# Feed-forward gate and up as seven block products, down in three passes, on a two-block network (one Trainium2 core)

## Chip, core and metric

The kernel runs on one core of a Trainium2 chip. The metric is the device time of one execution in microseconds (us). An execution's engines are TensorE (PE), VectorE (DVE), ScalarE (ACT), GpSimd (POOL) and SyncE (SP, which here issues DMAs).

## What is computed

The input is 1024 tokens of 1024 floats (fp32), and there are two blocks. The first has a mixer (a convolution branch and a recurrent branch, merged and multiplied by w_o) and a gated feed-forward part; the second has two further mixers and 32 experts. The part that the change touches, from the reference (D_FF is 2816):

```python
x = x + merged @ w_o[l]
h = rmsnorm(x, ln2_g[l])
x = x + (jax.nn.silu(h @ w_ffn_gate[l]) * (h @ w_ffn_up[l])) @ w_ffn_down[l]
return rmsnorm(x, final_g)
```

## The kernel before

**Numbers.** Each fp32 operand of a matrix product is held as a high and a low part of 12 bits (`split`: the high part is an ACT copy, L56, the low part a DVE subtraction, L57), and a product is three fp32r matmuls (`mm3`, L87 to L89: high x high, high x low, low x high). A weight tile of 1 MB is loaded by SP into one of two `raw` buffers, and its split units come from a pool of five.

**Stages.** `stage1` is the first mixer, in two halves of 512 tokens (`hf`); its last product, w_o, adds the residual and stores the sum x2 to DRAM (`x2d`). `prep` then norms token tiles of 128 (`norm`, L124 to L126, with `rstd`, whose power runs on POOL, L117) and transposes them (`to_T`, L135 on PE, L138 on ACT, L139 on DVE) to operands of 512 tokens, `xT` and `x2T`. `stage2` is the feed-forward part, `stage4` the mixers of the second block, `stage5` the experts.

**Feed-forward.** 2816 columns are 22 tiles of 128. `gates()` and `ups()` take two of them at a time: per column tile and token half one `col` of 8 k-tiles x 3 matmuls of 128x512, that is 96 per pair of tiles. The gate's tanh (L446, ACT), its product (L447, DVE) and the product with up (L462, DVE) give the hidden tile, which is split at once (L463 ACT, L464 DVE) and stays in SBUF. `down()` multiplies each pair of hidden tiles with two rows of w_ffn_down, for all eight token tiles and both halves of the columns, and L482 (DVE) adds each result to the residual `xh` in SBUF: 160 additions. The last two pairs go by halves of the tokens, with the final norm (`finish`, L489 and L491) and the next stage's transposes between them. The order of the work on each engine is set by the scheduler of the framework from the order in which the program is written.

```python
            sg = gates()
            for t in range(0, NFF - 4, 2):
                hid = ups(sg)
                sg = gates()
                down(hid, down_units(t), range(8))
```

Of the kernel before, what the change touches and what calls it, by code (L numbers as in the profile page):

```python
# [31 lines left out]
class Net:  # L32
# [39 lines left out]

    def n_units(self, w, r0, nk, c0):
        """Row tiles of w, 512 columns from c0, two row tiles a unit."""
# [9 lines left out]
    def mm3(self, out, w, x, first, last):  # L84
        """out += w^T x, both as (high, low) pairs; w is the one held in the array."""
# [5 lines left out]
    def col(self, ps, unit, xT, n0=0, n=HT):  # L91
        """ps [128 columns, n tokens] = unit^T xT"""
# [7 lines left out]
    def pair(self, slot, name):  # L100
        """A (high, low) pair [128, 8, 512] in one of the two large slots."""
# [8 lines left out]
    def rstd(self, pool, ssq, n, scale=1.0):  # L110
        """(scale * ssq / n + eps) ^ -0.5 for [128, m]"""
# [8 lines left out]
    def norm(self, pool, x, gB, out):  # L120
        """out = rmsnorm(x) * g for a natural tile [128, 1024]"""
# [7 lines left out]
    def to_T(self, psp, xn, dst, t0, nk=KD, k0=0, tag="tp"):  # L129
        """dst (high, low) [:, k, t0:t0+128] = xn[:, k*128:(k+1)*128]^T"""  # L130
# [10 lines left out]
    def rows_T(self, psp, wk, tmp, specs, name, tag="tp"):  # L141
        """Vectors of DRAM, as rows of 128, turned to columns: {name: [128, n] AP}."""
# [17 lines left out]
    def stage1(self):  # L160
        tc, nc, a = self.tc, self.nc, self.a
        self.x2d = self.dram.tile([S, D], F32, name="x2d")
        with ExitStack() as ctx:
# [3 lines left out]
            pst = ctx.enter_context(self.pool(name="s1pt", bufs=2, space=PSUM))  # L167

            def t(name):
                return wk.tile([P, HT], F32, tag="t", name=name, bufs=11)  # L170
# [49 lines left out]
            # softplus(-lambda)  # L220
# [6 lines left out]
            # block-diagonal maps of the heads 2c, 2c + 1 for c of a pair  # L227
# [11 lines left out]

            for hf in range(2):  # L240
                T0 = hf * HT

                # short convolution branch
                ya = self.pair(1 - hf, "ya")
                for c in range(0, 8, 2):
                    cs = []
                    for j, u in enumerate(self.t_units(w_in, [D + c * P, D + c * P + P])):
# [17 lines left out]
                    for j, u in enumerate(self.t_units(w_in, [c * P, c * P + P])):  # L265
# [3 lines left out]
                        self.put(ya, c + j, cs[j])  # L269

                if hf == 0:
                    self.route_const()
                pa = mid.tile([P, 8, HT], F32, tag="pa", name="pa")
# [12 lines left out]
                # recurrent branch  # L286
                yb = self.pair(1 - hf, "yb")
                for c in range(0, 8, 2):
# [25 lines left out]
                    def gates():  # L314
                        for j in range(2):
# [7 lines left out]
                            # x = -log a = 4 sp (1 + tr);  1 - a = (1 + e^-x) tanh(x / 2)  # L323
# [7 lines left out]
                        # sqrt(1 - a^2) = (1 + a) sqrt(tanh(x / 2))  # L331
# [23 lines left out]
                thb = mid.tile([P, 8, HT], F32, tag="thb", name="thb")  # L355
# [12 lines left out]
                # the next transposed input is made while the last product runs  # L368
                xT = self.pair(1 - hf, "xT")
                if hf == 0:  # L370
                    prep(lambda tt: load(a["x"][0, HT + tt * P:HT + (tt + 1) * P, :], nc.gpsimd), a["ln1_g"][0], xT)
                else:
                    prep(lambda tt: load(self.x2d[tt * P:(tt + 1) * P, :], nc.gpsimd), a["ln2_g"][0], xT)
                    x2n = mid.tile([P, 4, D], F32, tag="pa", name="x2n")
                for ch in range(2):
# [6 lines left out]
                    for tt in range(4):  # L382
                        r0 = T0 + tt * P
                        cs = slice(ch * 512, (ch + 1) * 512)
                        xr = x2n[:, tt, cs] if hf else t("xr")
# [3 lines left out]
            self.x2T = [xT, self.pair(1, "x2T")]  # L389
            prep(lambda tt: x2n[:, tt], a["ln2_g"][0], self.x2T[1])  # L390

    def put(self, dst, k, src):
        """dst (high, low) [:, k] = src"""
# [4 lines left out]
    def softplus(self, tmp, out, x, sgn, bias=0.0):  # L398
        """out = log(1 + exp(y)), y = sgn * x + bias; tmp() gives a tile like out."""
# [5 lines left out]
        # log1p(e) = 2 atanh(z), z = e / (2 + e) <= 1/3  # L405
# [11 lines left out]
    def stage2(self):  # L417
        tc, nc, a = self.tc, self.nc, self.a
        with ExitStack() as ctx:
            hp = ctx.enter_context(self.pool(name="s2hid", bufs=4))  # L420
            wk = ctx.enter_context(self.pool(name="s2wk", bufs=2))
            psp = ctx.enter_context(self.pool(name="s2ps", bufs=6, space=PSUM))
            pst = ctx.enter_context(self.pool(name="s2pt", bufs=2, space=PSUM))
            self.resc = ExitStack()
            self.res = self.resc.enter_context(self.pool(name="res", bufs=1, side="right"))
            res1 = ctx.enter_context(self.pool(name="res1", bufs=1, side="right"))
            self.x1h = self.res.tile([P, 4, D], F32, tag="xh", name="xh0")
            xh1 = res1.tile([P, 4, D], F32, name="xh1")
            xres = [self.x1h[:, t] for t in range(4)] + [xh1[:, t] for t in range(4)]
            self.x1d = self.dram.tile([HT, D], F32, name="x1d")  # L430
            xT = self.x2T
            for t in range(8):
                nc.gpsimd.dma_start(xres[t], self.x2d[t * P:(t + 1) * P, :])
            wd = a["w_ffn_down"][0]
            gg = self.t_units(a["w_ffn_gate"][0], [t * P for t in range(NFF)])
            gu = self.t_units(a["w_ffn_up"][0], [t * P for t in range(NFF)])

            def gates():
                sg = []
                for _ in range(2):  # L440
                    u = next(gg)
                    for hf in range(2):
                        ps = psp.tile([P, HT], F32, tag="acc", name="acc")
                        self.col(ps, u, xT[hf])
                        th = wk.tile([P, HT], F32, tag="th", name="th", bufs=4)
                        nc.scalar.activation(th, ps, AF.Tanh, scale=0.5)  # L446
                        nc.vector.scalar_tensor_tensor(th, th, 1.0, ps, op0=ALU.add, op1=ALU.mult)  # L447
                        sg.append(th)
                return sg

            def ups(sg):
                hid = []
                for j in range(2):
                    u = next(gu)
                    ht = hp.tile([P, 2, S], F32R, tag="hid", name="hid")
                    hid.append(ht)
                    for hf in range(2):
                        s = slice(hf * HT, (hf + 1) * HT)
                        ps = psp.tile([P, HT], F32, tag="acc", name="acc")
                        self.col(ps, u, xT[hf])  # L460
                        th = sg[2 * j + hf]
                        nc.vector.tensor_tensor(th, th, ps, ALU.mult)  # L462
                        nc.scalar.activation(ht[:, 0, s], th, AF.Copy)  # L463
                        nc.vector.tensor_tensor(ht[:, 1, s], th, ht[:, 0, s].bitcast(F32), ALU.subtract)  # L464
                return hid

            def down_units(t):
# [1077 lines left out]
```

## Time and profile before

| what | value |
|---|---|
| time, median of 3 runs | 3396.74 us (3393.51 to 3402.04) |
| span of the profiled execution | 3397.5 us |
| PE busy | 3230.0 us, 95% |
| DVE, ACT, POOL busy | 2072.2, 1419.9, 609.1 us |
| PE's granted clock, most slices | 1.0 |

The profiled execution is 0.8 us longer than the median of the runs; the page gives no time for it but its span. The stages follow one another; the feed-forward block fills about 950 to 1667 us. A busy share is a mean over all stages, so for each claim the rows of its own stretch are read.

### The profile page before, as it was taken

To read this page: it belongs to the slowest core of one execution; us is meant where nothing else is said; L and a number is where in the kernel's file an instruction comes from. 1 tells how busy PE (TensorE), PEld (TensorE's weight loads), DVE (VectorE), ACT (ScalarE), POOL (GpSimd) and SP (SyncE) were. 2 spreads that over 40 slices of the span, in tenths; PEclk is the share of its full clock that TensorE was granted. 3 is DMA by queue.
4 is the path that set the end of the run, shared out by engine and by line. 5 is a ranking of instruction groups with operands and counts; after the bars stand their busy time and mean duration, and the time that the engine had idled before them with its cause. 6 is when DMAs were issued, how large, how long until landed. Compare 5 with 4: busy or idle time off the path is not lost. (4 is left out here: it accounts for less than half of the span.)

```text
span 3397.5 us, 39631 instructions
## 1 busy us (share of the span) xinstructions
PE 3230.0 (95%) x15457; PEld 2661.3 (78%) x15457; DVE 2072.2 (61%) x2869; ACT 1419.9 (42%) x1954; POOL 609.1 (18%) x649
## 2 busy tenths in 40 slices
PE   8999999999999999999999999899999899999993
PEld 6887888877778888888777888777888778878772
DVE  5437544365544334333787665877656678888886
ACT  3227432255321111111343333443443378878873
POOL 0002210011210000000232111132112143334433
PEclk9999999999999999999999999999999899999996
DMA  4332433323431111111323323243332699969993
GB/s 154 99 100 85 145 118 99 99 85 117 136 118 50 50 50 38 62 50 35 105 88 106 103 91 92 73 145 109 103 109 93 230 322 384 381 256 389 368 349 155
DMA packets 313080, 487.81 MB, mean 144 GB/s; under 512 B 28400, under 2 KB 190460, under 8 KB 311868
## 3 DMA queue, kind: packets, MB, share of 16 engines
q1 hardware_dynamic: 291532, 427.02, 36.5%
q0 software_dynamic: 19488, 51.44, 4.2%
q10 hardware_dynamic: 1872, 6.82, 0.5%
q8 instruction: 122, 2.00, 0.2%
q14 instruction: 66, 0.54, 0.0%
HBM read 465.65 MB, written 36.34 MB: 148 GB/s over the span
## 5 line engine op out<-in xcount | busy, mean ns | idle before, releaser
L57 DVE TENSOR_TENSOR unit<-raw,unit 128x1024 fp32r<-128x1024 f32 x682 | 887.0, 1321 | 434.1 <-ACT unit L56 427.1
L56 ACT ACTIVATE unit<-raw 128x1024 fp32r<-128x1024 f32 x746 | 775.8, 1057 | 770.7 <-PE acc L89 689.5
L87 PE MATMUL acc<-xT,unit 128*128 128x512 f32 x1712 | 679.3, 397 | 0.1
L88 PE MATMUL acc<-xT,unit 128*128 128x512 f32 x1712 | 672.2, 393 | 0.0
L89 PE MATMUL acc<-xT,unit 128*128 128x512 f32 x1712 | 670.3, 392 | 0.0
L87 PEld LDWEIGHTS acc<-xT,unit 128*128 128x128 f32 x1712 | 323.7, 189 | 68.7 <-issue 1.2
L88 PEld LDWEIGHTS acc<-xT,unit 128*128 128x128 f32 x1712 | 323.4, 189 | 68.4 <-issue 3.6
L89 PEld LDWEIGHTS acc<-xT,unit 128*128 128x128 f32 x1712 | 323.2, 189 | 68.2 <-issue 1.0
L88 PE MATMUL gu<-unit,xT 128*128 128x512 f32 x512 | 207.3, 405 | 16.7 <-POOL unit L57 9.5
L87 PE MATMUL gu<-unit,xT 128*128 128x512 f32 x512 | 207.2, 405 | 1.1 <-ACT xT L138 0.8
L89 PE MATMUL gu<-unit,xT 128*128 128x512 f32 x512 | 204.5, 400 | 0.0
L88 PE MATMUL acc<-unit,xT 128*128 128x256 f32 (+1 forms) x640 | 196.4, 307 | 2.0 <-DVE unit L57 2.0
L87 PE MATMUL acc<-unit,xT 128*128 128x256 f32 (+1 forms) x640 | 193.9, 308 | 3.1 <-ACT xb L709 3.0
L89 PE MATMUL acc<-unit,xT 128*128 128x256 f32 (+1 forms) x640 | 195.4, 306 | 0.0
L57 POOL TENSOR_TENSOR unit<-raw,unit 128x1024 fp32r<-128x1024 f32 x64 | 157.7, 2464 | 156.8 <-issue 89.9
L482 DVE SCALAR_TENSOR_TENSOR xh<-acc,xh 128x512 f32<-128x512 f32 x160 | 110.4, 690 | 85.1 <-PE acc L89 84.5
L87 PE MATMUL acc<-unit,hid 128*128 128x512 f32 x352 | 137.3, 390 | 0.0
L89 PE MATMUL acc<-unit,hid 128*128 128x512 f32 x352 | 137.2, 390 | 0.0
L87 PE MATMUL acc<-x2T,unit 128*128 128x512 f32 x352 | 137.1, 389 | 0.1
L88 PE MATMUL acc<-unit,hid 128*128 128x512 f32 x352 | 137.1, 389 | 0.0
L88 PE MATMUL acc<-x2T,unit 128*128 128x512 f32 x352 | 136.9, 389 | 0.0
L89 PE MATMUL acc<-x2T,unit 128*128 128x512 f32 x352 | 136.9, 389 | 0.0
(425 smaller groups left out, 5641.0 us busy)
## 6 DMA issues: line engine op xcount, KB each, us to landing
raw<-in_w_in_dram SPq DMA_DIRECT2D x104, 1024.0 KB
raw<-in_exp_w_gate_dram SPq DMA_DIRECT2D x64, 1024.0 KB
raw<-in_exp_w_up_dram SPq DMA_DIRECT2D x64, 1024.0 KB
raw<-in_exp_w_down_dram SPq DMA_DIRECT2D x64, 1024.0 KB
raw<-in_w_ffn_gate_dram SPq DMA_DIRECT2D x11, 1024.0 KB
raw<-in_w_ffn_up_dram SPq DMA_DIRECT2D x11, 1024.0 KB
raw<-in_w_ffn_down_dram SPq DMA_DIRECT2D x11, 1024.0 KB
raw<-in_w_out_dram SPq DMA_DIRECT2D x9, 1024.0 KB
```

What stands on the lines that cost most here:

```text
L56: nc.scalar.activation(h, src, AF.Copy)
L57: (low or nc.vector).tensor_tensor(l, src, h.bitcast(F32), ALU.subtract)
L87: mm(out, w[0], x[0], start=first, stop=False)
L88: mm(out, w[0], x[1], start=False, stop=False)
L89: mm(out, w[1], x[0], start=False, stop=last)
L482: nc.vector.scalar_tensor_tensor(xs, ps, 0.5, xs, op0=ALU.mult, op1=ALU.add)
```

## The change

**Gate and up by block products.** The product of a pair of column tiles with all tokens is cut 2x2x2 (two halves of k, two column tiles, two token halves) and made from seven products of half the k each, instead of eight: sums of weight blocks (`b_blocks`, L459 to L471, five additions of 128x512 on POOL per pair) are multiplied with sums of token blocks, and the results are put together by DVE additions on 128x512 (`vadd`, L644). The seven are called m1 to m7; they take 7 x 4 x 3 = 84 matmuls. Some accumulate into a bank that another has filled (L642). The order of the steady loop: m1 and m6 of a pair, m4 of the pair before it (into the bank of its m7), m2, m3 of the pair before, m5, m7, with the splits of the next pair's weights between. `use` makes tanh and products (L659, L660, L663); the hidden tiles are stored to DRAM (`hidD`, by the ACT queue, 44 DMAs of 256 KB).

**Early tokens.** The first 512 tokens are normed, transposed and summed during the second half of stage 1 (`early`), and their six blocks are kept in DRAM (`eD`, 24 stores of 256 KB) and read back in stage 2 (six loads of 1 MB).

**w_o of the later tokens** moves to stage 2: eight PSUM banks for four token tiles x two column halves; k-tiles 0 to 3 for all of them first, then 4 to 7 tile by tile (`last`), each tile followed by its norm (`norm_a` to `norm_c`) and its transposes and sums (`turn`, L606 to L627; the low parts of the sums on POOL, L618).

**Down** comes after all of gate and up, in three passes over token tiles 0 to 2, 3 to 5 and 6 to 7: each accumulates all 22 k-tiles in PSUM, reads the hidden tiles and all of w_ffn_down again, and adds the residual once (L867, 16 additions). `finish` of a pass is followed by the transposes for stage 4 in the next.

```diff
-            def gates():
-                        self.col(ps, u, xT[hf])
-            def down(hid, us, tts):
-                        nc.vector.scalar_tensor_tensor(xs, ps, 0.5, xs, op0=ALU.mult, op1=ALU.add)
...
+        def sums(names):
+            t, T, V = t2()
+            if names == ("T2", "T1"):
+                g(V, B12, B11, ALU.subtract)
+                g(T, B22, V, ALU.subtract)
+            elif names == ("T3", "T4"):
+                g(T, B22, B12, ALU.subtract)
+                g(V, B21, T, ALU.subtract)
+                g(V, V, B11, ALU.subtract)
...
+                def m1(m):
+                    m.A = acc()
+                    prod(m.A, m.b["B11"], x["A11"], True)
+                    m.s1 = st("s1")
+                    nc.scalar.activation(m.s1, m.A, AF.Copy)
+                def m2(m):
+                    prod(m.A, m.b["B21"], x["A12"], False)
+                    m.use(0, m.A)
+                def m4(m):
...
+                        prod(m.B, m.b["T4"], x["A22"], False)
+                        vadd(m.s1, m.s1, m.B)
+                        m.use(2, m.s1)
+                def m5(m):
+                    m.C = acc()
+                    prod(m.C, m.b["T1"], x["S1"], True)
+                def m6(m):
+                    m.B = acc()
+                    prod(m.B, m.b["T2"], x["S2"], True)
+                    m.u2 = st("u2")
+                    vadd(m.u2, m.s1, m.B)
+                def m7(m):
+                    prod(m.B, m.b["T3"], x["S3"], False)
+                    m.u3 = st("u3")
+                    vadd(m.u3, m.s1, m.B)
...
+                    vadd(m.u3, m.u3, m.C)
+                    m.use(3, m.u3)
+                def m3(m):
+                    prod(m.C, m.b["B22"], x["S4"], False)
+                    vadd(m.u2, m.u2, m.C)
+                    m.use(1, m.u2)
...
+            last(2, 0)
+            t = turn(0)
+            for _ in t:
+                pass
+            last(2, 1)
+            rs[2] = norm_a(2)
+            last(3, 0)
+            t = turn(1)
+            next(t)
+            norm_b(2)
+            next(t)
+            norm_c(2, rs[2])
+            last(3, 1)
...
+            for n in range(3, NFF + 1):
+                q = Mat(n, ths) if n < NFF else None
+                m.m1()
+                m.m6()
+                if p:
+                    p.m4()
+                m.split()
+                m.m2()
+                if p:
+                    p.m3()
+                if q:
+                    q.split(2)
+                m.m5()
+                if q:
+                    q.split()
+                m.m7()
+                p, m = m, q
+            p.m4()
+            p.m3()
...
+            for tts in ((0, 1, 2), (3, 4, 5), (6, 7)):
+                n = len(tts)
+                accs = [[acc() for _ in range(2)] for _ in tts]
+                for f in range(0, NFF, 2):
+                    hr = hp.tile([P, 2, n * P], F32, tag="hr", name="hr", bufs=2)
+                    nc.sync.dma_start(hr, self.hidD[f * P:(f + 2) * P, t0:t0 + n * P].rearrange("(k p) t -> p k t", p=P))
+                    raw = self.raw_p.tile([P, 2, D], F32, tag="raw", name="raw")
+                    nc.sync.dma_start(raw, wd[f * P:(f + 2) * P, :].rearrange("(k p) c -> p k c", p=P))
```

**The order on the engines.** DVE before, in the feed-forward loop, from one pair's down splits over the products of up to the gates of the next:

```order
L57 TENSOR_TENSOR unit_6905<-raw_6844,unit_6905 128x1024
L57 TENSOR_TENSOR unit_6966<-raw_6964,unit_6966 128x1024
L462 TENSOR_TENSOR th_6496<-th_6496,acc_6728 128x512
L464 TENSOR_TENSOR hid_6727<-th_6496,hid_6727 128x512
L462 TENSOR_TENSOR th_6524<-th_6524,acc_6756 128x512
L57 TENSOR_TENSOR unit_6969<-raw_6964,unit_6969 128x1024
L464 TENSOR_TENSOR hid_6727<-th_6524,hid_6727 128x512
L462 TENSOR_TENSOR th_6555<-th_6555,acc_6788 128x512
L464 TENSOR_TENSOR hid_6787<-th_6555,hid_6787 128x512
L462 TENSOR_TENSOR th_6583<-th_6583,acc_6816 128x512
L57 TENSOR_TENSOR unit_7102<-raw_7100,unit_7102 128x1024
L464 TENSOR_TENSOR hid_6787<-th_6583,hid_6787 128x512
```

DVE in the changed kernel, one pair of the steady loop (`raw` is a weight tile as loaded, `tw` sums of weight blocks; `unit` from either is a split; `acc` is a PSUM bank; s1, u2 and u3 are partial results):

```order
L644 TENSOR_TENSOR u3_7455<-s1_7356,acc_7358 128x512
L644 TENSOR_TENSOR u3_7455<-u3_7455,acc_7427 128x512
L660 SCALAR_TENSOR_TENSOR th_7458<-th_7458,u3_7455 128x512
L644 TENSOR_TENSOR u2_7498<-s1_7483,acc_7485 128x512
L644 TENSOR_TENSOR s1_7356<-s1_7356,acc_7358 128x512
L57 TENSOR_TENSOR unit_7516<-raw_7334,unit_7516 128x512
L660 SCALAR_TENSOR_TENSOR th_7513<-th_7513,s1_7356 128x512
L663 TENSOR_TENSOR th_7403<-th_7403,acc_7470 128x512
L57 TENSOR_TENSOR unit_7549<-raw_7461,unit_7549 128x1024
L644 TENSOR_TENSOR u2_7371<-u2_7371,acc_7427 128x512
L57 TENSOR_TENSOR unit_7552<-tw_7463,unit_7552 128x1024
L660 SCALAR_TENSOR_TENSOR th_7546<-th_7546,u2_7371 128x512
```

Between the splits stand additions of partial results, which were not there before; two of a pair's splits read what POOL has added.

POOL in the changed kernel, at the norms of the later tokens' tiles (`rs_r`, L117, is the power of one tile's norm, tiles 0 to 2 in this order; L618 makes the low part of one sum; L470 and L471 are weight sums):

```order
L117 TENSOR_TENSOR rs_r_6124<-rs_v_6122,mhalf_77 128x1
L117 TENSOR_TENSOR rs_r_6159<-rs_v_6157,mhalf_77 128x1
L571 DMA x2_5951<-in_x_dram 128x1024
L618 TENSOR_TENSOR s2_5923<-sum_6184,s2_5923 128x4x128
L618 TENSOR_TENSOR s3_5924<-sum_6185,s3_5924 128x4x128
L618 TENSOR_TENSOR xe_5921<-sum_6186,xe_5921 128x4x128
L470 TENSOR_TENSOR tw_6440<-raw_6083 128x512
L471 TENSOR_TENSOR tw_6440<-tw_6440,raw_6083 128x512
L618 TENSOR_TENSOR s2_5923<-sum_6240,s2_5923 128x4x128
L117 TENSOR_TENSOR rs_r_6249<-rs_v_6247,mhalf_77 128x1
L618 TENSOR_TENSOR s3_5924<-sum_6241,s3_5924 128x4x128
L618 TENSOR_TENSOR xe_5921<-sum_6242,xe_5921 128x4x128
```

In the kernel before only norms stood there; the power of the third tile now stands behind six instructions of 128x512.

DVE in the changed kernel, at the end of gate and up (u3_9089 is the last pair's m7, acc_9000 its bank; hid and unit with raw_9159 and raw_9208 are operands of the down product):

```order
L57 TENSOR_TENSOR unit_9164<-raw_9159,unit_9164 128x1024
L644 TENSOR_TENSOR u2_8895<-u2_8895,acc_8951 128x512
L57 TENSOR_TENSOR unit_9167<-raw_9159,unit_9167 128x1024
L660 SCALAR_TENSOR_TENSOR th_9061<-th_9061,u2_8895 128x512
L849 TENSOR_TENSOR hid_9161<-hr_9157,hid_9161 128x768
L57 TENSOR_TENSOR unit_9213<-raw_9208,unit_9213 128x1024
L849 TENSOR_TENSOR hid_9210<-hr_9206,hid_9210 128x768
L644 TENSOR_TENSOR u3_9089<-s1_8998,acc_9000 128x512
L644 TENSOR_TENSOR u3_9089<-u3_9089,acc_9064 128x512
L663 TENSOR_TENSOR th_8982<-th_8982,u3_9089 128x512
```

The additions of the last pair stand behind five splits for the down product, which did not exist apart before.

## Rows read from the trace of the kernel before

**Rows 1.** The page's first part: busy us, share of the span, number of instructions.

```profile
span 3397.5 us, 39631 instructions
...
PE 3230.0 (95%) x15457; PEld 2661.3 (78%) x15457; DVE 2072.2 (61%) x2869; ACT 1419.9 (42%) x1954; POOL 609.1 (18%) x649
```

**Rows 2.** Windows: length and busy us (instructions) by engine, granted clock, DMA share, GB/s.

```profile
core 0: us, PE busy (x) PEld busy (x) DVE busy (x) ACT busy (x) POOL busy (x), PEclk, DMA share, GB/s
950.00:1640.00 690.00, 690.00 (x3045) 571.33 (x3044) 270.93 (x365) 116.98 (x159) 6.85 (x13) 1.00 0.16 54
850.00:900.00 50.00, 48.95 (x226) 39.94 (x225) 31.67 (x33) 18.99 (x26) 15.19 (x19) 1.00 0.46 146
900.00:950.00 50.00, 45.21 (x216) 37.15 (x217) 25.80 (x34) 17.35 (x26) 11.83 (x21) 1.00 0.43 147
2800.00:2900.00 100.00, 100.00 (x465) 81.23 (x464) 87.09 (x84) 85.55 (x100) 39.97 (x22) 1.00 1.03 384
```

**Rows 3.** Groups of the feed-forward block: count | busy us, mean ns | idle before.

```profile
L87 PE MATMUL acc<-x2T,unit 128*128 128x512 f32 x352 | 137.1, 389 | 0.1
...
L482 DVE SCALAR_TENSOR_TENSOR xh<-acc,xh 128x512 f32<-128x512 f32 x151 | 104.3, 690 | 84.2 <-PE acc L89 83.8
L57 DVE TENSOR_TENSOR unit<-raw,unit 128x1024 fp32r<-128x1024 f32 x61 | 73.8, 1221 | 12.3 <-ACT unit L56 12.3
...
L56 ACT ACTIVATE unit<-raw 128x1024 fp32r<-128x1024 f32 x61 | 63.5, 1055 | 262.0 <-PE acc L89 262.0
...
L464 DVE TENSOR_TENSOR hid<-th,hid 128x512 fp32r<-128x512 f32 x44 | 30.3, 688 | 15.7 <-ACT hid L463 15.7
...
L463 ACT ACTIVATE hid<-th 128x512 fp32r<-128x512 f32 x44 | 27.4, 624 | 108.0 <-DVE th L462 98.5 <-DVE mlast L601 4.8 <-issue 4.7
L446 ACT ACTIVATE th<-acc 128x512 f32<-128x512 f32 x44 | 26.3, 597 | 187.4 <-PE acc L89 187.4
L491 DVE SCALAR_TENSOR_TENSOR xh<-xh,rs_r,gB 128x1024 f32<-128x1024 f32 x3 | 3.9, 1284 | 2.1 <-POOL rs_r L117 2.1
```

**Rows 4.** Timeline of PE in the first stage: start us, us, instruction.

```profile
119.64 0.39 PE L87 MATMUL acc<-xT,unit 128*128 128x512 f32 x1
...
123.94 0.39 PE L88 MATMUL acc<-xT,unit 128*128 128x512 f32 x1
```

**Rows 5.** PE's waits from 860 to 960 us: total us, times, longest.

```profile
PE tp L135 <- DVE xn L126: 3.3, 2, 2.4
PE tp L135 <- DVE x2T L139: 1.6, 1, 1.6
PE tp L135 <- DVE xT L139: 0.8, 1, 0.8
```

**Rows 6.** Timeline of PE at the ramp, and where the next stage begins.

```profile
902.21 1.07 PE L135 MATMUL tp<-ident,xn 128*128 128x128 f32 x8 [2.40 <-DVE xn L126]
...
1667.14 0.39 PE L89 MATMUL acc<-unit,hid 128*128 128x512 f32 x1
1667.37 0.39 PE L87 MATMUL acc<-xT,unit 128*128 128x512 f32 x1
```

**Rows 7.** Timeline of DVE and POOL in the mixer's last columns.

```profile
881.94 2.04 DVE L57 TENSOR_TENSOR unit<-raw,unit 128x1024 fp32r<-128x1024 f32 x1 [0.41 <-ACT unit L56]
...
881.62 1.29 POOL L365 TENSOR_TENSOR thb<-thb,pa 128x512 f32<-128x512 f32 x1 [4.15 <-DVE thb L364]
```

**Rows 8.** Durations of line L117 on POOL: ns min/median/max, first and last start.

```profile
L117 POOL TENSOR_TENSOR rs_r<-rs_v,mhalf x64: 538/555/1590, 7.4 to 3391.4; 128x1 f32<-128x1 f32 x64
```

**Rows 9.** DMA issues from 870 to 950 us: KB, median us to landing.

```profile
xh<-x2d POOLq DMA_DIRECT2D x8, 512.0 KB, 6.7
```

**Rows 10.** Timeline of PE in the experts' stretch.

```profile
2850.22 0.40 PE L87 MATMUL dn<-unit,hT 128*128 128x512 f32 x1
...
2858.39 0.40 PE L89 MATMUL gu<-unit,xT 128*128 128x512 f32 x1
```

**Rows 11.** Durations of line L57 on DVE: ns min/median/max, first and last start.

```profile
L57 DVE TENSOR_TENSOR unit<-raw,unit x682: 1158/1221/4124, 18.6 to 3341.2; 128x1024 fp32r<-128x1024 f32 x171
```

More of the change, by code (lines that the diff above doesn't have):

```diff
@@ L366, in stage1 @@
                     self.put(mg, j, thb[:, j])
[L369 to L374, printed above, removed]
+                if hf:
+                    break
+                xT = self.pair(1, "xT")
+                prep(lambda tt: load(a["x"][0, HT + tt * P:HT + (tt + 1) * P, :], nc.gpsimd), a["ln1_g"][0], xT)
                 for ch in range(2):
@@ L388, in stage1, with quad, blk, b_blocks @@
                         nc.gpsimd.dma_start(self.x2d[r0:r0 + P, cs], xr)
-            self.x2T = [xT, self.pair(1, "x2T")]
-            prep(lambda tt: x2n[:, tt], a["ln2_g"][0], self.x2T[1])
+            ptc.close()
+        self.mg = mg
+    def quad(self, x, kh):
+        return x[0][:, 4 * kh:4 * kh + 4], x[1][:, 4 * kh:4 * kh + 4]
+    def blk(self, pool, tag):
+        t = pool.tile([P, 2, 4, HT], F32R, tag=tag, name=tag)
+        return t[:, 0], t[:, 1]
+    def b_blocks(self, tw, w, c, first):
+        nc = self.nc
+        raw = self.raw_p.tile([P, KD, 2 * P], F32, tag="raw", name="raw")
+        nc.sync.dma_start(raw, w[:, c:c + 2 * P].rearrange("(k p) c -> p k c", p=P))
+        B11, B12 = raw[:, 0:4, 0:P], raw[:, 0:4, P:]
+        B21, B22 = raw[:, 4:8, 0:P], raw[:, 4:8, P:]
+        g = nc.gpsimd.tensor_tensor
+        out = {}
+        def t2():
+            t = tw.tile([P, 2, 4, P], F32, tag="tw", name="tw")
+            return t, t[:, 0], t[:, 1]
+        def split(src, names):
+            u = self.split(src, [4 * len(names), P])
+            for j, n in enumerate(names):
+                out[n] = (u[0][:, 4 * j:4 * j + 4], u[1][:, 4 * j:4 * j + 4])
+        def sums(names):
[7 more added lines that the diff above has]
+                g(V, V, B11, ALU.subtract)
+            elif names == ("T4", "T1"):
+                g(V, B12, B11, ALU.subtract)
+                g(T, B21, B22, ALU.subtract)
+                g(T, T, V, ALU.add)
+            else:
+                g(V, B22, B12, ALU.subtract)
+                g(T, V, B11, ALU.add)
+            return t.rearrange("p a k c -> p (a k) c"), names
+        cols = (raw[:, :, 0:P], ("B11", "B21"))
+        def walk(todo):
+            for q in todo:
+                split(*q)
+                yield
+        if first:
+            one = sums(("T4", "T1"))
+            def later():
+                split(*one)
+                yield
+                split(*cols)
+                yield
+                split(*sums(("T2", "T3")))
+                yield
+                split(B22, ("B22",))
+                yield
+            return out, later()
+        return out, walk([cols, sums(("T2", "T1")), sums(("T3", "T4")), (B22, ("B22",))])
@@ L451, in ups @@
[L451 to L465, printed above, removed]
@@ L517, in stage4 @@
+        psc.close()
     def stage4(self):
```

334 lines of the change are left out of this document (266 added, 68 removed).

## The prediction, made blind

> **What bounds the kernel now.** I read the page's busy times first: TensorE (PE) is busy for 3230.0 of 3397.5 us, 95%, while VectorE (DVE), ScalarE (ACT) and GpSimd (POOL) have 61, 42 and 18% [rows 1]. Such shares are means over stages, so I read the stretches next. From 950 to 1640 us, which is the feed-forward block alone, PE is busy for 690.00 of 690 us at a granted clock of 1.00 (the 2.4 GHz level), DVE for 271, ACT for 117, POOL for 7, and the DMA share is 0.16 [rows 2]. Nothing else comes near, so a matmul less is time less there. What one matmul is worth is not its 389 ns of "mean busy" [rows 3], since matmuls overlap: from the one that starts at 119.64 to the one at 123.94 there are 19 steps in 4.30 us, 0.2263 us each [rows 4], and the 3045 instructions of the 690 us give 690/3045 = 0.2266. I take 0.2266. The Trainium skill (TensorE: Matmul & The Clock Gate) states 512/2.4 GHz and some 2.5 ns, 215.7 ns, from start to start of warm matmuls; the rows differ, they decide, and by the page's figure the first term below would be 57.
>
> Ahead of that stretch PE is not full: 48.95 and 45.21 of two 50-us windows [rows 2]. The waits there are transposes that wait for the norms of the later tokens: 3.3 + 1.6 + 0.8 = 5.7 us [rows 5]. Behind it there is no hole: the last down matmul starts at 1667.14 and the next stage's first at 1667.37 [rows 6].
>
> **The change, term by term.**
> 1. *Gate and up products.* Before, a pair of column tiles takes 2 columns x 2 token halves x 8 k x 3 = 96 matmuls; now 7 block products x 4 k x 3 = 84. There are 22 pairs (11 gate, 11 up): 22 x 12 = 264 matmuls of 128x512 fewer. The orders agree: w_o (384), down (1056) and the transposes keep their counts. 264 x 0.2266 = **-59.8 us**, all of it on the path, as PE is full.
> 2. *What the block products ask of the others, per pair, for which PE now takes 84 x 0.2266 = 19.0 us.* DVE: three splits of 128x1024 (1.22), one of 128x512 (0.69), five adds (0.69) and four uses (L660/L663, 0.69) = 3.66 + 0.69 + 3.45 + 2.76 = 10.6 us. ACT: 3 x 1.06 + 0.62, one s1 copy and two tanh in the mean (0.60 each) = 5.6 us, and two DMA issues. These durations are from [rows 3]. POOL: five sums of 128x512; the nearest row is the same engine's add of that shape, 1.29 [rows 7], so 6.4 us. Each is under 19.0, so on average **0**. But the two engines disturb each other: where POOL's L365 ran for 1.29 us from 881.62, a DVE split that takes 1.22 in the mean took 2.04 [rows 7], 0.82 more. Five such sums add at most 5 x 0.82 = 4.1 us to DVE: 14.7 of 19.0. The Trainium skill (SBUF — State Buffer, Who interferes with whom) says that a DVE instruction with two SBUF inputs contends with a POOL instruction that reads SBUF, by an exclusive lock; the trace agrees, and with every overlap paid in full DVE and POOL together would hold 10.6 + 6.4 = 17.0 us, still under 19.0. It is the rule that speaks most against this change.
>  Averages are not enough, since single results have due times. By the order, a pair's first split stands on DVE behind about three other instructions and its unit is asked for one pair later; I count about 2.8 us to spare for it, and 3.6 to 3.9 for the sums' splits and for the bank of m7, which p.m4 fills again. One overlap costs 0.82, so two to three fit. Bounds per pair: 0 and 1 us (an overlap more than fits, 0.82, rounded up), so 0 to 22. I take 0, since the sums are spread over the pair (order, DVE below).
> 3. *The first pairs*, where weights come before the pipeline is full: one to two splits late at 1.22: **+1.5**, bounds 0 and 5.
> 4. *The w_o ramp.* The stalls of before, 5.7, go, as those transposes go [rows 5]: **-5.7**. New ones come: turn(0) to turn(3) wait for the norms of the four later tiles, whose pow stands in POOL's queue behind the sums' lows (order, POOL). From the first L618 on, six POOL instructions of 1.29 and the pow of 0.55 [rows 8] stand ahead of norm_c of tile 2: 8.3 us, after a copy, an add and a copy of about 1.9, and then 1.28 for norm_c itself (L491's row in [rows 3]): 11.5. PE has 48 matmuls and 8 transposes (1.1, [rows 6]) meanwhile, 12.0 us. That just fits, and each DVE/POOL overlap eats 0.82; turn(3) and the low of A11, which g.m1 needs, stand as close. Bounds: 0 (all fits) and 13 (four turns with 3.3 each, what the two of before lost together). I take **+6.5**, near before's own ramp of 5.7.
> 5. *The early tokens' blocks.* 24 stores of 256 KB and six loads of 1 MB. They lie under stage 1 and w_o; in the experts' stretch the queues move 384 GB/s with PE busy for 100.00 of 100 us [rows 2], and here it is 13 MB more over some 300 us. **0**; bounds 0 and 4, one late load.
> 6. *Gate/up to down.* m7 of the last pair leaves a bank that p.m4 accumulates into; the DVE add that reads it first (L644 on u3) now stands behind splits of the down product that wait for fresh loads (order, the seam). Nearest rows: a split of 1.22 and an add of 0.69. **+2.2**; bounds 0.7 (the add alone) and 6.7 (a 512 KB load of before lands 6.7 us after its issue [rows 9]).
> 7. *Down in three passes.* w_ffn_down is loaded three times (33 MB for 11) and the hidden blocks are read again. A step of 36 matmuls takes 8.2 us for 1.44 MB, 178 GB/s, one of 24 in the last pass 5.4 us for 1.3 MB, 243 GB/s; 384 was sustained [rows 2]. DVE's split of the step is 2 x 1.22 + 1.03 = 3.5 (1.03 is 1.5 times the 128x512), ACT's 3.0 by the same reckoning. The 160 additions of L482, 110 us of DVE, become 16: no gain, as PE's windows are full with them [rows 2, 3]. **0**; bounds 0 and 4 (a late first load at each of two pass borders).
>
> Sum: -59.8 + 1.5 - 5.7 + 6.5 + 2.2 = -55.3. The profiled execution, 3397.5 us, stands 0.8 above the median of the runs, 3396.74; so 3397.5 - 55.3 = 3342.2 for a like execution, 3341.4 against the median. I forecast **3342 us**.
>
> **Rivals.**
> - *Late units in every pair* (chance 0.16): DVE splits stretched by POOL come after their slack. Price: 1 us x 22 pairs = 22, so 3364. For it: the 2.04 us splits [rows 7]; against: 14.7 of 19.0 us.
> - *Matmuls at a wider step* (0.07): in the experts' stretch, at clock 1.00 too, 35 matmuls from 2850.22 to 2858.39 need 8.17 us, 0.2334 each [rows 10], and I don't know why. There DMA and DVE are busy as they are not in the feed-forward block, and now both rise. If gate, up and down went at that step: (1848 + 1056) x 0.0068 = +20, so 3362.
> - *DVE and POOL become the bound, and it is slower* (0.04): a split (L57) took up to 4.12 us somewhere in the trace [rows 11]. With one such split in each pair, 2.9 us longer than the mean, and the 2.8 us to spare already spent on the 4.1 of the sums, PE would wait 2.9 us in each of 22 pairs: +64, so 3406, 9 above before. It decides from about 2.5 us of waiting per pair, which is 55 us in 22 pairs. For it: POOL does almost nothing in this block now, 6.85 us in 690, and gets 142; against: DVE's and POOL's sum of 17.0 is under 19.0.
> - *The down product becomes DMA-bound* (0.03): at the 54 GB/s the queues move in this block [rows 2] it would, but that is demand and not a limit; if they reached only 200 GB/s, the 11 steps of the last pass lose 1.1 us each, 12 in all: 3354.
> - *The ramp costs nothing, or no first-pair stalls* is in the likeliest case's bounds: 3342.2 - 9.5 = 3333.
>
> **How the numbers follow.** The likeliest case, PE full with the four small terms, has 0.70 and its own range is 3333 to 3354: terms 3, 4 and 6 at their low ends, and terms 3 to 7 half-way to their high ones (7.3 + 4). The runs shown reach 3.2 below their median, so the low end is 3330. The wider step, the DMA-bound case and the late units at 1 us lie by 3366; the units that are later still and the slower rival are left out. So 3330 to 3366. What a measurement of this kernel tells from no change is about 0.3%, 10.2 us: 3387 to 3407. Faster by more than that: all cases but the slower rival and a share of the late units that are twice as late: 0.92. Within: 0.05. Slower: 0.03 (of the slower rival's 0.04, most; the rest lies within).
>
> **What would show it.** In the profile of the changed kernel the windows of the gate/up part hold PE at 50.00 of 50 with a DVE share near 0.6 and POOL near 0.35; a pair takes 19.0 us, by the start of one pair's first product to the next one's; PE's waits in it name no DVE or POOL split. The ramp shows some 6 us of waits of L606's transposes and of the first products for DVE and POOL; the down part shows steps of 8.2 us and no idle PE beyond 2 us at the two pass borders. Wrong would be: PE waits of a microsecond or more in each pair on DVE unit L57 (first rival), steps of 0.233 us with no waits at all (second), PE busy under 45 of 50 in the gate/up windows (third), DMA named as what PE's or the splits' waits ended on in the down part (fourth).

## The result and the profile after

The changed kernel takes 3356.11 us (median of 4 runs, 3355.08 to 3358.11) against 3396.49 for the kernel before: a ratio of 0.9878, 95% interval 0.9864 to 0.9892, or 40.4 us less. The forecast was 3342, in a range of 3330 to 3366. The direction and the range held; the time is 14 us above the forecast. The page of the changed kernel, against [rows 1]:

```profile
span 3354.6 us, 39834 instructions
...
PE 3178.5 (95%) x15193; PEld 2608.5 (78%) x15193; DVE 2221.8 (66%) x2928; ACT 1520.8 (45%) x2069; POOL 825.0 (25%) x758
```

15457 - 15193 = 264 matmuls are gone, as reckoned. The span is 42.9 us shorter. Its windows (columns as in [rows 2]): gate and up, the w_o ramp, the passage from gate/up to down, down, and experts:

```profile
1000.00:1350.00 350.00, 350.00 (x1518) 285.08 (x1517) 200.16 (x234) 99.98 (x127) 135.89 (x87) 1.00 0.25 82
920.00:960.00 40.00, 36.37 (x168) 29.65 (x167) 32.12 (x39) 20.43 (x34) 26.54 (x22) 0.96 0.15 58
...
1370.00:1376.00 6.00, 5.57 (x17) 4.46 (x18) 2.49 (x5) 1.52 (x2) 0.53 (x1) 0.64 0.63 228
...
1400.00:1550.00 150.00, 150.00 (x675) 124.55 (x674) 73.29 (x78) 58.57 (x72) 6.49 (x9) 1.00 0.52 184
2756.00:2856.00 100.00, 97.80 (x448) 78.20 (x449) 98.13 (x83) 82.08 (x96) 43.11 (x21) 1.00 1.02 370
```

The kernel before over the same 350 us, which are feed-forward in both:

```profile
1000.00:1350.00 350.00, 350.00 (x1546) 289.83 (x1545) 140.97 (x185) 56.09 (x74) 0.00 (x0) 1.00 0.15 49
```

PE is full in both, but fits 1518 matmuls into the time where 1546 went before: 0.2306 us each instead of 0.2264. A busy engine is not an engine at its old pace; "350.00 of 350" hides this, the count beside it shows it. PE's waits from 900 to 1400 us, against [rows 5]:

```profile
PE acc L642 <- DVE u L644: 5.9, 2, 5.5
PE acc L606 <- DVE x L597: 2.9, 2, 2.6
PE acc L88 <- DVE mg L623: 0.7, 1, 0.7
```

None of them recurs from pair to pair. The differences from the forecast can be read off stage by stage. From the start of w_o for the later tokens to the first matmul of the second block the kernel before needs 886.09 to 1667.37, the changed one 890.25 to 1620.97: 50.6 us less, of which 4.2 are the early transposes now done ahead of it. So 46.4 us are gained up to there, 8.9 short of 55.3, and behind it, where the code is the same, 3.5 are lost: the second mixer takes 1.4 us more, the experts 2.4 (622.9 and 625.3 us from the first gathered tokens' transpose to the last dn matmul), and 0.3 come back at the end.

**The step.** The products of one pair in the changed kernel (PE's timeline; L642 rows hold twelve matmuls, of the others the first of twelve is shown):

```profile
1057.35 0.40 PE L87 MATMUL acc<-s,unit 128*128 128x512 f32 x1
...
1060.17 2.92 PE L642 MATMUL acc<-xe,unit 128*128 128x512 f32 x12
1062.93 2.88 PE L642 MATMUL acc<-mg,unit 128*128 128x512 f32 x12
1065.65 2.88 PE L642 MATMUL acc<-xe,unit 128*128 128x512 f32 x12
1068.37 0.40 PE L87 MATMUL acc<-s,unit 128*128 128x512 f32 x1
...
1071.18 2.96 PE L642 MATMUL acc<-s,unit 128*128 128x512 f32 x12
1073.98 0.40 PE L87 MATMUL acc<-mg,unit 128*128 128x512 f32 x1
...
1076.74 0.40 PE L87 MATMUL acc<-s,unit 128*128 128x512 f32 x1
```

From start to start, the products on mg and xe at 1062.93 and 1065.65 take 2.72 us (0.2267 a matmul), those on the S tiles (1057.35, 1068.37, 1071.18) 2.82, 2.81 and 2.80 (0.2350 to 0.2333). The two others take 2.76 (1060.17 on xe, 1073.98 on mg), and each of them stands right behind a product on an S tile. A pair takes 1076.74 - 1057.35 = 19.39 us where 19.03 were reckoned. In the built program mg and xe start at multiples of 64 bytes in SBUF, S1 to S3 at 32 past one; and the same holds for the wide steps of the kernel before [rows 10]: its xT5 and hT5 start 32 past.

**The passage to down.** PE, DVE and ACT of the changed kernel there (timeline, one after the other):

```profile
1370.43 7.52 PE L642 MATMUL acc<-xe,unit 128*128 128x512 f32 x24 [5.49 <-DVE u L644]
1377.79 0.39 PE L87 MATMUL acc<-unit,hid 128*128 128x512 f32 x1
...
1365.86 0.96 DVE L849 TENSOR_TENSOR hid<-hr,hid 128x768 fp32r<-128x768 f32 x1 [3.57 <-ACT hid L848]
1366.81 1.23 DVE L57 TENSOR_TENSOR unit<-raw,unit 128x1024 fp32r<-128x1024 f32 x1
1368.82 0.96 DVE L849 TENSOR_TENSOR hid<-hr,hid 128x768 fp32r<-128x768 f32 x1 [0.79 <-ACT hid L848]
1369.70 0.68 DVE L644 TENSOR_TENSOR u<-s,acc 128x512 f32<-128x512 f32 x1
...
1364.98 0.84 ACT L848 ACTIVATE hid<-hr 128x768 fp32r<-128x768 f32 x1 [4.04 <-DMA hr<-hidD]
```

The add that PE waits for stands on DVE behind two splits of hidden tiles, and those wait, by ACT, for their load. PE stands for 5.49 us, and then its clock is lower (0.64 in the mean from 1370 to 1376 us): the 24 matmuls of m4 and m3 take 7.36 us instead of 5.4.

**The experts.** DVE's splits there, in the kernel before and in the changed one (groups of instructions, columns as in [rows 3]):

```profile
L57 DVE TENSOR_TENSOR unit<-raw,unit 128x1024 fp32r<-128x1024 f32 x320 | 425.8, 1371 | 53.9 <-ACT unit L56 47.3 <-PE tp L135 2.7
```

```profile
L57 DVE TENSOR_TENSOR unit<-raw,unit 128x1024 fp32r<-128x1024 f32 x320 | 482.9, 1553 | 33.6 <-ACT unit L56 30.5 <-PE tp L135 2.7
```

The same 320 splits take 57 us longer. DVE is busy for 98 of 100 us, and one expert takes 18.78 us in the middle of the stage where it took 18.11 (from one expert's first transpose to the next one's). Two such starts in the kernel before, and two in the changed one:

```profile
2828.44 1.03 PE L135 MATMUL tp<-ident,xg 128*128 128x128 f32 x8
2846.55 1.03 PE L135 MATMUL tp<-ident,xg 128*128 128x128 f32 x8
```

```profile
2821.16 1.03 PE L135 MATMUL tp<-ident,xg 128*128 128x128 f32 x8
2839.93 1.03 PE L135 MATMUL tp<-ident,xg 128*128 128x128 f32 x8
```

The stage as a whole is only 2.4 us longer, since the second expert and the last ones take less than before; why they do was not looked into.

### The profile page after: what moved, and what is told of

Read it like the earlier page. It is cut to its first block, busy times and chain, and to the rows that moved or that the text cites. A ratio compares the mean times of both kernels' runs of the same rounds, so it can differ in the third digit from the quotient of the medians.

```text
span 3354.6 us, 39834 instructions
## 1 busy us (share of the span) xinstructions
PE 3178.5 (95%) x15193; PEld 2608.5 (78%) x15193; DVE 2221.8 (66%) x2928; ACT 1520.8 (45%) x2069; POOL 825.0 (25%) x758
## 5 line engine op out<-in xcount | busy, mean ns | idle before, releaser
L57 DVE TENSOR_TENSOR unit<-raw,unit 128x1024 fp32r<-128x1024 f32 x726 | 989.9, 1384 | 490.2 <-ACT unit L56 486.3
L56 ACT ACTIVATE unit<-raw 128x1024 fp32r<-128x1024 f32 (+1 forms) x790 | 813.7, 1045 | 749.9 <-PE acc L89 524.7
L87 PE MATMUL acc<-xT,unit 128*128 128x512 f32 x1360 | 542.8, 400 | 0.6 <-ACT xT L138 0.6
L88 PE MATMUL acc<-xT,unit 128*128 128x512 f32 x1360 | 536.0, 394 | 0.0
L89 PE MATMUL acc<-xT,unit 128*128 128x512 f32 x1360 | 534.3, 393 | 0.0
L87 PEld LDWEIGHTS acc<-xT,unit 128*128 128x128 f32 x1360 | 257.9, 190 | 55.1 <-issue 1.0
L88 PEld LDWEIGHTS acc<-xT,unit 128*128 128x128 f32 x1360 | 257.5, 189 | 54.3 <-issue 3.3
L89 PEld LDWEIGHTS acc<-xT,unit 128*128 128x128 f32 x1360 | 257.3, 189 | 54.0 <-issue 1.0
L57 POOL TENSOR_TENSOR unit<-raw,unit 128x1024 fp32r<-128x1024 f32 x64 | 176.5, 2758 | 273.6 <-issue 221.0
L88 PEld LDWEIGHTS gu<-unit,xT 128*128 128x128 f32 x512 | 96.9, 189 | 55.2 <-DVE unit L57 27.3
L87 PEld LDWEIGHTS acc<-unit,xT 128*128 128x128 f32 x640 | 122.1, 191 | 11.1 <-ACT xb L1065 4.7
L642 PE MATMUL acc<-xe,unit 128*128 128x512 f32 x504 | 123.7, 396 | 5.9 <-DVE u L644 5.9
L88 PEld LDWEIGHTS acc<-unit,xT 128*128 128x128 f32 x640 | 122.3, 191 | 8.2 <-DVE unit L57 2.5
```

The costliest lines, as they stand in the source:

```text
L56: nc.scalar.activation(h, src, AF.Copy)
L57: (low or nc.vector).tensor_tensor(l, src, h.bitcast(F32), ALU.subtract)
L87: mm(out, w[0], x[0], start=first, stop=False)
L88: mm(out, w[0], x[1], start=False, stop=False)
L89: mm(out, w[1], x[0], start=False, stop=last)
L642: nc.tensor.matmul(ps, w[i], v[j], start=False, stop=(k == 3 and i == 1), skip_group_check=True)
```

## The experiments

All times are medians against the kernel before on the same chip, whose own medians were 3396.70, 3397.26 and 3397.74 in the three batches. The changed kernel was not run again beside them, so a difference from its 3356.11 is one between batches; and the intervals of the single edits of it (runs 1 to 4 and 6, and the sums on DVE in run 5) all overlap its own, 0.9864 to 0.9892. What one such edit does is therefore read from its trace, and the difference in time only goes with it. The kernel before with fillers (run 4), the doubled sums (run 5) and the four edits together (run 7) are clear of the noise.

**1. The S tiles, 32 bytes on.**

```diff
+            xp = ctx.enter_context(self.pool(name="xpad", bufs=1, side="right"))
+            nc.vector.memset(xp.tile([P, 8], F32, name="xpad"), 0.0)
             xs = ctx.enter_context(self.pool(name="xs", bufs=1, side="right"))
```

> The changed kernel, with a 32-byte filler tile ahead of S1, S2 and S3, so that these three start at a multiple of 64 bytes (before: 32 past one). In the changed kernel's trace the products that read S1 to S3 step by 0.2342 us, those on mg and xe by 0.2267 to 0.2300. Theory (the start address of the moving operand sets the step): the S products fall to 0.2267, 3 of 7 products, 792 matmuls x 0.0075 = 5.9 us less, and the matmuls of mg that follow an S product fall too; the whole about 6 to 8 us faster than the changed kernel, near 3349. Rival (DVE's and POOL's SBUF traffic beside the S products sets the step): the step stays at 0.234 and the time at 3356.

3353.61 us, 0.9868 (0.9851 to 0.9884). The window, and a part of one pair's products (L644 is the L642 of the changed kernel, two lines on):

```profile
1000.00:1350.00 350.00, 350.00 (x1529) 286.62 (x1528) 192.82 (x236) 100.60 (x127) 138.68 (x87) 1.00 0.25 82
...
1063.17 2.88 PE L644 MATMUL acc<-mg,unit 128*128 128x512 f32 x12
1065.89 2.88 PE L644 MATMUL acc<-xe,unit 128*128 128x512 f32 x12
1068.62 0.40 PE L87 MATMUL acc<-s,unit 128*128 128x512 f32 x1
...
1071.38 2.91 PE L644 MATMUL acc<-s,unit 128*128 128x512 f32 x12
1074.12 0.40 PE L87 MATMUL acc<-mg,unit 128*128 128x512 f32 x1
```

The S product that took 2.81 now takes 2.76; the step of the window falls from 0.2306 to 0.2289, 1848 x 0.0017 = 3.1 us, half of what was expected. The start address costs about 0.0045 a matmul on an S tile (0.2342 to 0.2298 in the mean of the window), not 0.0075. The rival fails in its prediction of an unchanged step; run 5 takes it up again. The rest of the way to 0.2266, some 4.2 us, remains: the three products on S tiles and the two right behind one still take 2.75 to 2.77 us in the mean, and the two at 2.72 are those that neither read an S tile nor follow one. So the rest still goes with the S tiles, and I have not found what it is. In the built program S1 to S3 now start 64 bytes past a multiple of 128, mg and xe at a multiple of 128; no run moved them there.

**2. Own banks for the last pair's m4 and m3.**

```diff
-                        prod(m.B, m.b["T4"], x["A22"], False)
-                        vadd(m.s1, m.s1, m.B)
+                        m.D = acc()
+                        prod(m.D, m.b["T4"], x["A22"], True)
+                        vadd(m.s1, m.s1, m.B)
+                        vadd(m.s1, m.s1, m.D)
```

> The changed kernel, with m4 and m3 of the last pair in PSUM banks of their own, and one more DVE addition each. Theory (the last pair's m4 waits for DVE's read of m7's bank, which stands behind the first splits of down): the wait of 5.5 us before m4 goes, and with it the stretch at the lower clock, 1.9 us; the down product's first matmul follows m3 with less than 1 us between; 6 to 7.5 us faster, near 3349. Rival (the wait only moves, because down's first units wait for the load of the hidden tiles all the same): down's first matmul waits about 3 us, and 2 to 4 us are gained.

3348.69 us, 0.9859 (0.9842 to 0.9876): 7.4 less than the changed kernel. Down begins at 1369.58 instead of 1377.79. Part of the wait moved on: down's banks are waited for, with two smaller waits,

```profile
1373.03 0.50 PE L87 MATMUL acc<-unit,hid 128*128 128x512 f32 x1 [1.93 <-DVE u L644]
1375.37 0.50 PE L87 MATMUL acc<-unit,hid 128*128 128x512 f32 x1 [0.68 <-DVE u L644]
```

so that the second block begins 5.2 us earlier in the trace; the other 2.3 us of the shorter span lie behind it, where the edit changes nothing (the second mixer, 1056.5 us in the changed kernel, takes 1053.8 to 1058.2 in the runs that leave it alone). The wait and the lower clock in front of m4 are gone, as the theory has it, and the rival has its share: 2.6 us of waiting moved on.

**3. The count of splits ahead of the experts, +4, then +2.** `split` counts its calls, and in the experts' stage every sixth goes to POOL. The first of the two runs rests on a miscount of mine (it left out the 44 splits of sums); it is a run at a third place.

```diff
         self.wctx.close()
+        self.nsplit += 2
```

> The changed kernel, with 4 added to the count of splits ahead of the experts, so that every sixth split that POOL does there falls on the same units as in the kernel before (746 splits there, 790 now: two off in six). In the changed kernel an expert takes 18.8 us in the middle of that stage, before 18.1, and DVE is busy for 98 of 100 us against 87. Theory (the shifted choice puts POOL's split beside DVE's in a worse place): an expert takes 18.1 us again, DVE falls to 87%, and about 10 us are gained in that part, 2 to 9 in the whole, near 3350. Rival (the state of the loads or chance sets it): 18.8 stays and the time with it, 3356.

3355.57 us, 0.9877 (0.9860 to 0.9893). The 18.60 us that the next expectation gives for an expert is not one pace: in this trace an expert takes 18.11 us from the third to the eleventh and mostly 18.7 to 18.8 from the twelfth on, with POOL's splits on the same units in all of them (an expert has 12 splits).

```profile
2819.15 1.03 PE L135 MATMUL tp<-ident,xg 128*128 128x128 f32 x8
2837.26 1.03 PE L135 MATMUL tp<-ident,xg 128*128 128x128 f32 x8
...
2910.93 1.04 PE L135 MATMUL tp<-ident,xg 128*128 128x128 f32 x8
2929.69 1.04 PE L135 MATMUL tp<-ident,xg 128*128 128x128 f32 x8
```

> The changed kernel, with 2 added to the count of splits ahead of the experts. The gate/up part splits 88 units where the kernel before split 44, and down 66 for 22, so the count is 88 higher, 4 off in six; adding 4 more, in the run before this one, made another wrong place, and 2 makes it that of the kernel before. Theory (which splits POOL takes sets how long POOL and DVE block each other): an expert takes 18.1 us (18.78 in the changed kernel, 18.60 with 4 added), DVE's mean split falls from 1.55 to 1.37 us, and 5 to 15 us are gained in the experts' stage. Rival (loads or chance): 18.6 to 18.8 again.

3350.23 us, 0.9855 (0.9838 to 0.9871), 5.9 less than the changed kernel; an expert 18.11 us as before, and the experts' stage 617.2 us instead of 625.3. Its splits and a window of its experts:

```profile
L57 DVE TENSOR_TENSOR unit<-raw,unit 128x1024 fp32r<-128x1024 f32 x320 | 424.2, 1366 | 51.1 <-ACT unit L56 45.2 <-PE tp L135 2.7
...
2756.00:2856.00 100.00, 100.00 (x469) 81.42 (x468) 87.28 (x85) 85.62 (x100) 39.56 (x22) 1.00 1.02 388
```

With the count of before, the pace of an expert, DVE's share and its mean split are those of before. The 88 more splits in gate, up and down had moved POOL's splits to other units, in a stage that the change does not touch. Every kernel here with the changed kernel's count takes 18.8 us for an expert in the middle of the stage, every one with the count of before 18.1 or less. At the third place, 4 added, one trace holds both paces, so there the place alone does not decide; what makes it change over is open.

**4. yT, xT5 and hT5, 32 bytes on,** in the changed kernel and in the kernel before. The fillers move the other tiles of the same two pools by 32 bytes as well.

```diff
+            p5 = ctx.enter_context(self.pool(name="pad5", bufs=1))
+            nc.vector.memset(p5.tile([P, 8], F32, name="pad5"), 0.0)
             wk = ctx.enter_context(self.pool(name="s5wk", bufs=2))
```

> The changed kernel, with 32-byte filler tiles in the second mixer and in the experts' stage, so that yT, xT5 and hT5 (weights of the array or moving operand there) start at multiples of 64 bytes; the count of splits is left as it is. Theory (a start address off by 32 makes the step 0.2334, whichever operand has it): gu, dn and yT products step by 0.2267. The second mixer gains up to 768 x 0.0067 = 5 us; the experts gain little while DVE is busy for 98 of 100 us there: 0 to 5. Rival (the busy engines and DMAs set the step of the experts): gu and dn stay at 0.2334, nothing gained, 3356.

3354.31 us, 0.9874 (0.9857 to 0.9890). The gu matmuls step by 0.2284 (0.2332 in the changed kernel), but an expert still takes 18.77: DVE is the bound there, and the gain turns into PE's waiting. The second mixer is 4.2 us shorter in the trace (1052.3 us, 1.5 under the shortest of the runs that leave it alone).

```profile
2756.00:2856.00 100.00, 96.24 (x453) 78.48 (x452) 98.03 (x80) 82.65 (x97) 47.79 (x22) 1.00 1.02 377
```

> The kernel before, with the 32-byte fillers of the second mixer and the experts (yT, xT5, hT5 at multiples of 64 bytes). There an expert is bound by PE: 18.1 us, 72 matmuls at 0.2334. Theory (the start address sets the step, some 0.0047 per matmul by the two runs so far): gu steps 0.2284 or less, an expert 72 x 0.0047 = 0.34 us shorter, 32 experts 11 us, the mixer 2 to 4: 3382 to 3387. Rival (the step of the experts is from contention, the fillers do nothing): 3397.

3386.18 us, 0.9963 (0.9948 to 0.9977): the kernel before is 11.1 us faster by 32 bytes. An expert takes 17.73 us, gu steps by 0.2281; in the trace the experts' stage is 9.5 us shorter and the second mixer 6.6, while 2.6 are lost ahead of them, where nothing was moved.

```profile
2800.00:2900.00 100.00, 100.00 (x475) 83.15 (x474) 89.37 (x86) 87.17 (x102) 41.23 (x23) 1.00 1.03 388
```

DMA, DVE, ACT and POOL are as busy as in [rows 2], and PE does 475 matmuls in the 100 us instead of 465. So it is the start address of these tiles, not the traffic, that made that step wide.

**5. The weight sums on DVE, and twice on POOL.**

```diff
-        g = nc.gpsimd.tensor_tensor
+        g = nc.vector.tensor_tensor
```

> The changed kernel, with the five sums of weight blocks of a pair on DVE instead of POOL. Theory (gate/up is bound by PE, DVE has the room: 10.6 + 5 x 0.69 = 14.0 of 19.2 us per pair): PE full in the gate/up windows, no waits per pair, time within 3 us of the changed kernel. Rival (DVE with some splits late becomes the bound): PE waits on DVE unit L57 in each pair, 1 us or more, 22 or more in all. The ramp may gain or lose 3 us, as the norms of the later tiles leave POOL's queue.

3358.56 us, 0.9877 (0.9861 to 0.9893), 2.4 more. DVE goes from 200 to 237 us in the window and PE keeps its 1518 matmuls; no wait in the pairs. The same 1518 matmuls with POOL idle and DVE busier also mean that the wide step of gate and up, the unexplained part included, is not from POOL's traffic, and that more of DVE's does not widen it.

```profile
1000.00:1350.00 350.00, 350.00 (x1518) 284.97 (x1517) 237.31 (x321) 99.81 (x126) 0.00 (x0) 1.00 0.25 82
```

> The changed kernel, with each of POOL's weight-block sums issued twice (the in-place ones subtract twice, so another sum is computed). POOL then has 12.9 us per pair, and DVE with POOL, one after the other, 10.6 + 12.9 = 23.5 of 19.2 us. Theory (their blocking is partial, only where two-input DVE instructions and POOL overlap): PE stays full or waits under 1 us a pair, 0 to 20 us slower. Rival (they exclude each other for all of their time): PE waits (23.5 - 19.2) = 4.3 us a pair, some 95 us slower.

3409.02 us, 1.0034 (1.0023 to 1.0046). Most of this lies elsewhere, 37.8 us in the experts' stage (663.1 us instead of 625.3): the other sums change the hidden values and so the routing, and one expert runs a second block of tokens, which the changed kernel does not (33 x 8 transposes of gathered tokens, and a 17 us wait for the gather). The places that count are gate/up and the ramp:

```profile
1000.00:1350.00 350.00, 348.37 (x1509) 283.29 (x1508) 232.42 (x238) 101.28 (x127) 276.06 (x183) 1.00 0.25 82
900.00:970.00 70.00, 54.98 (x235) 45.10 (x233) 31.83 (x41) 22.40 (x35) 43.18 (x35) 0.88 0.31 116
...
L135 PE MATMUL tp<-ident,xg 128*128 128x128 f32 x264 | 37.4, 284 | 24.5 <-DMA xg<-h2d,ov_r 17.0 <-DMA xg<-h2d,sidx 7.5
```

PE loses 1.6 us of 350 with POOL at 276, so full exclusion (95 us) is out; the ramp loses 16.5 (m1 of the first pair starts at 969.66 instead of 953.17). POOL's sums have room in the pairs and none in the ramp.

**6. The lows of the ramp on DVE.**

```diff
-                    nc.gpsimd.tensor_tensor(l, q, f(h), tt_)
+                    nc.vector.tensor_tensor(l, q, f(h), tt_)
```

> The changed kernel, with the low parts of the later tiles' sums (L618, 12 of them) on DVE instead of POOL. Theory (the transposes of tiles 2 and 3 wait because the power of their norm stands behind lows and weight sums in POOL's queue, and because POOL and DVE block each other): the waits of L606's transposes fall from 2.9 to under 1 us, PE's clock stays at 2.4 GHz there, and 2 to 5 us are gained. Rival (DVE is the one that is full at the ramp: 12 x 0.69 = 8.3 us more on it in some 30 us): the waits grow to 4 to 8 us.

3359.38 us, 0.9884 (0.9868 to 0.9899): no gain. The waits of the transposes are 3.1 us (2.9 before the edit), and m1 starts 1.0 us earlier, at 952.17. The clock from 920 to 960 is 1.00, where the changed kernel had 0.96:

```profile
920.00:960.00 40.00, 36.60 (x175) 29.65 (x174) 34.62 (x52) 21.05 (x35) 9.10 (x11) 1.00 0.18 66
```

But that window shows 0.91 to 1.00 in runs that leave the ramp alone (0.91 in the run with 2 added, 1.00 in that with yT, xT5 and hT5 moved), so the 1.00 is not shown to be the edit's. Neither theory is borne out: the waits neither fall nor grow. That POOL's queue and DVE's take turns as the last is a guess.

**7. The four edits together,** and with the lows.

> The changed kernel with four of the edits above: S1 to S3, yT, xT5 and hT5 at multiples of 64 bytes, own banks for the last pair's m4 and m3, and 2 added to the count of splits ahead of the experts. Theory (the costs are independent): 3356 less 3 (S tiles), 6 (tail), 6 (count) and 11 (yT, xT5, hT5, as in the kernel before with the same fillers): 3330, 1.9 to 2.1% under the kernel before. Rival (DVE or the DMAs bind the experts' stage once PE is quicker there): the 11 falls to 3 to 5, 3336.

3332.09 us (3326.09 to 3333.29), 0.9798 (0.9784 to 0.9813): 65.7 us, 2.0%, under the kernel before, and faster than both kernels. The costs add up to within 3 us: 3356.1 - 2.5 - 7.4 - 5.9 - 11.1 = 3329, with the 11.1 from the kernel before (in the changed kernel the same fillers gave 1.8, as DVE bound the experts there). An expert takes 17.69 us, and the rival's bound by DVE or the DMAs does not come.

> The kernel with the four edits, and besides the low parts of the later tiles' sums on DVE. Theory: it moves against the kernel with the four edits as the run with the lows alone moves against the changed kernel: 2 to 5 us faster. Rival: 2 to 5 us slower, since DVE is full at the ramp.

3331.98 us, 0.9800 (0.9784 to 0.9816): the same; neither expectation came.

## Why the prediction was right, and what was off

The bound was read rightly: PE was full before and is full after, 264 matmuls went and the time fell with them. But 3356 stands 2 us above the likeliest case's own range (3333 to 3354); the stated range holds it because the rivals widened it to 3366. The points of the sum, by its numbers:

| term | forecast | measured in the trace |
|---|---|---|
| 1 matmuls | -59.8 | -59.8, less 7.3 for the wider step (3.1 start address, 4.2 open) |
| 2 DVE, POOL in the pairs | 0 | 0, no waits |
| 3 first pairs | +1.5 | +0.4 |
| 4 ramp | -5.7 + 6.5 | -5.7 + 5.2 (waits 3.6, lower clock 1.6) |
| 6 passage to down | +2.2 | +7.4 (wait 5.5, lower clock 1.9) |
| 7 down in three passes | 0 | 0, PE 150.00 of 150 |
| stages behind | none given | +3.5 |

Up to the second block these make -45.2, where the trace has -46.4. Of the 3.5 behind, the 1.4 of the second mixer lie within its scatter from run to run. The lower clock of term 4 is an estimate, 0.04 of the 40 us window.

- **Term 1** had the count right and the worth of a matmul a little off. I took the step of the matmuls that go, and never asked at what step those that stay would run. The rival of a wider step came true in part: for the three products on S tiles and, less, for the two right behind one, not for down. The reason was not the one I gave, that DMA and DVE are busy there: for most of the experts' wider step and for 3.1 of the 7.3 us it is where the tile starts (runs 1 and 4), and for the rest it is open, with POOL's traffic ruled out (run 5). I had its rows at hand [rows 10] and wrote that I did not know why; I could have compared the start addresses of the tiles in the two stretches.
- **Term 2** held, with its reason. DVE and POOL do block each other: in the gate/up window of the changed kernel single sums take 1.3 to 2.2 us on POOL, and a use of two SBUF tiles 1.19 on DVE instead of 0.69,

```profile
L460 POOL TENSOR_TENSOR tw<-raw,tw 128x512 f32<-128x512 f32 x17 | 37.6, 2210 | 1.3
...
L660 DVE SCALAR_TENSOR_TENSOR th<-th,u 128x512 f32<-128x512 f32 x18 | 21.4, 1190 | 6.3 <-ACT th L659 6.3
```

 while additions that read one operand from PSUM stay at 0.69. With POOL idle (run 5, the sums on DVE) the same use takes 0.69 again:

```profile
L660 DVE SCALAR_TENSOR_TENSOR th<-th,u 128x512 f32<-128x512 f32 x19 | 13.1, 688 | 1.5 <-ACT th L659 0.7
```

 But the units have time to spare, even with the sums doubled (run 5). The rivals of late units and of DVE and POOL as the bound did not come.
- **Term 4** came near in part by luck: I took a price near that of the old ramp, all of it waits, and the 5.2 are waits of 3.6 and a lower clock that I had not counted.
- **Term 6** is the one that was mis-sized. I had the right add behind the right splits, but priced the splits' own time and not the load they wait for, though I had it as the upper bound (6.7). And I left out what a wait of that length costs behind it: the clock.
- **What was missing** is the experts' stage. The change alters how many splits are counted ahead of it, and that picks POOL's splits there; run 3 shows 18.11 and 18.78 us an expert for two places, and both paces at a third. It costs 8.1 us of the experts' stage (625.3 against 617.2 with the count of before); only 2.4 of them show against the kernel before, whose stage takes 622.9, since the changed kernel is 5.7 us quicker there otherwise. The forecast took the stages behind as unchanged because their code is.
- The down product is not bound by its DMAs: three passes run with PE full. The early blocks cost nothing that shows.

## What to carry to other kernels

When an edit removes work from a full engine, price what stays at its new operands and places too: count instructions per window, since a full engine at a wider step looks the same by its busy share. Follow every counter and every address that the edit shifts into later stages, for they can take back what a stage has gained. Where an engine waits at a seam, ask what the instructions in front of the awaited one are themselves waiting for.

## What the runs showed of the hardware

- A 128x512 matmul whose moving operand (S1 to S3) or whose weights (xT5, hT5) start 32 bytes past a multiple of 64 in SBUF took 0.2332 to 0.2350 us from start to start; moved to a multiple of 64 it took 0.2281 to 0.2300, while those on mg and xe that follow no S product took 0.2267. In the kernel before, two fillers of 32 bytes are worth 11.1 us.
- After a wait of 5.49 us the granted clock was 0.64 in the mean from 1370 to 1376 us, between the levels of 1.2 and 2.4 GHz, and 24 matmuls took 1.9 us longer. The wait of 2.40 us in the kernel before [rows 6] had left the window around it at 1.00 [rows 2]; one of 2.60 in the changed kernel's ramp came with 0.96 over 40 us, and in the run with yT, xT5 and hT5 moved one of 3.3 there came with 1.00. So in these runs the length of a wait of about 3 us does not tell what the clock does behind it.
- Which splits POOL takes beside DVE changed DVE's mean split in the experts' stage from 1.37 to 1.55 us at the same number of them (320).
